# One decoder-block kernel, seven edits joined: input preparation, norm steps, scaled rows, `w_down` rows, strided transposes, and a wait at the seam to the experts

## The chip, the cores and the metric

The kernel runs on one core of a Trainium2 chip. The time is device microseconds (us) of one execution; a measurement is the median of several runs. A profile is one execution of its own, recorded instruction by instruction. Engines: PE is TensorE, DVE is VectorE, ACT is ScalarE, POOL is GpSimd, SP issues most DMAs. ACT and POOL issue some too.

## What is computed

One decoder layer on x of 1024 tokens by 1024 channels, all in float32:

```python
h = rms_norm(x, attn_norm_g)
proj = h @ w_in                                   # 1024 x 4608: conv, q, k, v, two gates
conv_out = silu(layer_norm(conv31(a * sigmoid(gate))))       # 512 channels, 31 taps
attn_out = rms_norm((softmax(q1 k1) - lam * softmax(q2 k2)) @ v)   # 4 heads, causal
merged = gates[0] * (conv_out @ w_conv_out) + gates[1] * (attn_out @ w_attn_out)
x = x + merged @ w_out
h2 = rms_norm(x, ffn_norm_g)
# router: best of 4 groups, best 2 of its 8 experts; so 2048 rows spread over 32 experts
for e in range(32):
    y[rows_e] += w_e * ((silu(h2[rows_e] @ w_gate[e]) * (h2[rows_e] @ w_up[e])) @ w_down[e])
return x + y
```

Each expert has 6 MB of weights (`w_gate`, `w_up`, `w_down`, 2 MB each), 201 MB in all.

## The kernel before

Every large matmul is done on operands cut in two: `split` (L92) writes a high part on ACT (L93) and the rest on DVE (L94), and `mm3` multiplies three times (L98 to L100). So PE runs three matmuls for each product, and every operand costs an ACT and a DVE instruction.

**Input preparation and attention.** x comes in eight tiles of 128 tokens. For each tile, ACT squares it (`prep_a`, L194), DVE takes the inverse root in a chain of small instructions (`rsqrt`, L65 to L75), POOL multiplies the tile by the gain (`prep_g`, L202), DVE scales an identity by the inverse root (`prep_s`, L207), and PE multiplies the tile by that diagonal, which transposes and scales it at once (`prep_b`, L218, two groups of four blocks). A loop over units U (4 heads x 8 tiles and seven more) then projects one tile (24 matmuls into `pq`) and interleaves scores and values of earlier units. The order on PE and ACT is the order of the code in this part; a string `plan` says where the transposes of the next tile (`p`, `P`) stand among the eight projection steps (digits). In the first unit, POOL also makes the low parts of two of the four weight chunks. ACT evacuates the end of a projected tile into `rq` (L269).

**Convolution and gates.** The 31 taps run on DVE while PE does the gates. Between the gates stand the steps of the layer norm: `norm_stats` (four groups of transposes, L615) and `norm_silu` (four groups, L632), for each half of the tokens, through a ring of two PSUM tiles that ACT empties.

**Output projection and routing.** For two halves of 512 columns and eight token tiles, PE projects into `px`, DVE adds the residual (L801), POOL multiplies by the gain (`scaled`, L815, into `uu`), and an ACT DMA writes `uu` to DRAM as `h2d`. `scaled` also permutes the columns (it reads every fourth one), so that the gathered rows later match the weights' layout. In the second half the router runs in groups of tiles: a chain of some 35 DVE instructions whose `oh`, `ohb` (L956, L957) PE needs (L961). DVE also makes the low part `ml` of the next tile.

**Seam and experts.** The last group gives `idx` (L999). Then POOL gathers each expert's rows (L1002, an indirect DMA whose descriptors POOL writes), PE transposes them (`x_front`, L1013), and for each expert: gate and up projections, `hidden`, a transpose of the result (`hid_t`, L1041), the down projection and a scatter-add (L1055). Weights come by 1 MB DMAs on SP's queue (`chunk_dma`, L1066) into a ring of 12 buffers, with at most five loads in flight once the ring has been filled; ACT and DVE split each buffer (`ch` 1.92 us, `cl` 2.29 us), which frees it. A chunk of `w_gate` or `w_up` is one piece of 8 KB for each partition, a chunk of `w_down` two pieces of 4 KB.

Of the kernel before, what the change touches and what calls it, by code (L numbers as in the profile page):

```python
# [49 lines left out]
class Block:  # L50
# [132 lines left out]

    def xload(self, tb):
        xf = self.i["x"].rearrange("o t d -> (o t) d")
        self.nc.sync.dma_start(self.xts[:, tb % 4], xf[tb * P:(tb + 1) * P])

    def prep_a(self, *tbs):
        nc, xp = self.nc, self.xp
        n = len(tbs)  # L190
        ss = xp.tile([P, 2], F32, name="ss", bufs=3)[:, :n]
        rr = xp.tile([P, 2], F32, name="rr", bufs=3)[:, :n]
        for u, tb in enumerate(tbs):
            nc.scalar.activation(self.xmisc[:, 1], self.xts[:, tb % 4], AF.Square, accum_out=ss[:, u:u + 1])  # L194
        self.rsqrt(xp, rr, ss, n, 1.0 / D, f"xn{n}")
        for u, tb in enumerate(tbs):
            self.xr[tb] = rr[:, u:u + 1]

    def prep_g(self, tb):
        xt = self.xts[:, tb % 4]  # L200
        self.xg[tb] = xg = xt if tb else self.xmisc[:, 3]
        self.nc.gpsimd.tensor_tensor(xg, xt, self.gb, op=ALU.mult)  # L202

    def prep_s(self, tb):
        c = (tb % 2) * P
        self.dg[tb] = dg = self.xmisc[:, 3, c:c + P] if tb else self.xmisc[:, 2, 7 * P:]
        self.nc.vector.tensor_scalar(dg, self.ident, self.xr[tb], None, op0=ALU.mult)  # L207
# [5 lines left out]
    def prep_b_(self, tb, kk):  # L213
# [19 lines left out]
    def attention(self):  # L233
# [169 lines left out]
        with tc.manual_schedule(engines={E_.PE, E_.Activation}):  # L403
            self.xload(0)
            nc.sync.dma_start(self.gb, row_bcast(i["attn_norm_g"], D))
            wload(0, 0)
            self.xload(1)
            wload(0, 1)
            wload(0, 2)
            self.xload(2)  # L410
            wload(0, 3)
            self.xload(3)
            self.consts_load()
            self.xr, self.xg, self.dg = {}, {}, {}
            self.prep_g(0)
            self.prep_a(0)
            self.prep_s(0)
            self.prep_a(1)
            self.prep_g(1)
            wsplit(0, 0)  # L420
            self.prep_b(0, 0)
            self.prep_b(0, 4)
            self.prep_s(1)
            wsplit(0, 1, nc.gpsimd)
            wsplit(0, 2)
            self.prep_a(2)
            self.prep_g(2)
            wsplit(0, 3, nc.gpsimd)
            for U in range(NU + 7):
# [16 lines left out]
                if pj:  # L446
# [3 lines left out]
                    if h == 0 and tb + 4 < NT:  # L450
                        self.xload(tb + 4)
                    if h == 0 and 0 < tb < NT - 1:
                        self.prep_s(tb + 1)
# [38 lines left out]
                plan = "0p12cP3a4qk56Q7" if nxt else "012c3a4qk5Q67"  # L492
                for c in plan:
                    if c.isdigit():
                        step(int(c))
                    elif c == "p" and nxt:
                        self.prep_b(nxt, 0)
                        if U == 0:
                            self.prep_a(3)
# [22 lines left out]
                    elif c == "k" and U == 1:  # L522
# [83 lines left out]
    def norm_stats(self, th):  # L606
        nc, cv = self.nc, self.cv
        mv = cv.tile([P, 4, 2], F32, name="mv", bufs=2)
        z = [self.yp.tile([P, KW - 1 + T], F32, name="yy", bufs=2) for _ in range(2)]
        self.zs = zs = [z[t // 2][:, t % 2 * 512:(t % 2 + 1) * 512] for t in range(4)]  # L610
        for t, zt in enumerate(zs):
# [4 lines left out]
            nc.scalar.activation(zt, pt.rearrange("p a b -> p (a b)"), AF.Copy)  # L616
            st = cv.tile([P, 6], F32, name="st", bufs=2)
            nc.vector.bn_stats(st, zt)
            nc.vector.bn_aggr(mv[:, t], st)
        rr = cv.tile([P, 4], F32, name="crr", bufs=2)  # L620
        self.rsqrt(cv, rr, mv[:, :, 1], 4, 1.0, "cn")
        for t in range(4):
            nc.vector.tensor_scalar(zs[t], zs[t], mv[:, t, 0:1], rr[:, t:t + 1], op0=ALU.subtract, op1=ALU.mult)

    def norm_silu(self, th):
        nc = self.nc
        sl = slice(th * 512, (th + 1) * 512)
        for cb in range(NCB):
# [66 lines left out]

    def merge_conv(self, fills, stop, steps):
# [4 lines left out]
        for j in range(ND - 2):  # L701
            Wg = self.gate_load(CG0 + j * P)
            for th in range(2):
                self.gate(Wg, th, s2[th][:, j])
            self.pin = self.last_split
            self.fill(fills if j + 1 < stop else 99)
            for f, th in steps.get(j, ()):
                f(th)
        Wg = [self.gate_load(CG0 + j * P) for j in (ND - 2, ND - 1)]
        for th in range(2):  # L710
            for q in range(2):
                self.gate(Wg[q], th, s2[th][:, ND - 2 + q])
            if th == 0:
                for f, t in steps.get(ND - 1, ()):
                    f(t)
# [14 lines left out]
        for th in range(2):  # L730
            for j in range(ND):
                if th == 0 and j + 2 < ND:
                    Wo.append(wload(j + 2))
                if (th, j) == (0, 2):
                    self.norm_split(1)
# [3 lines left out]
                nc.vector.tensor_tensor(mg, mg, sg, op=ALU.add)  # L739

# [27 lines left out]
    def out_proj(self):  # L768
# [5 lines left out]
        for n in range(2):  # L774
# [6 lines left out]
            for tb in range(NT):  # L781
# [24 lines left out]
                self.scaled(uu, xt, gb2)  # L806
# [5 lines left out]

    def scaled(self, uu, xt, gb2):
        by = lambda a: a.rearrange("t (p k) -> t k p", k=4)
        self.nc.gpsimd.tensor_tensor(uu.rearrange("t (k p) -> t k p", k=4), by(xt), by(gb2), op=ALU.mult)  # L815

    def out_last(self, px, mh, ml, W, xt, prev, gb2):
# [30 lines left out]
        self.scaled(uu, xt, gb2)  # L848
# [473 lines left out]
```

## Time and profile before

| what | value |
|---|---|
| median of three runs | 1435.72 us (1428.46 to 1436.32) |
| the profiled execution | 1441.21 us |
| its span, first to last instruction | 1439.5 us |
| PE, DVE, ACT, POOL busy | 94%, 76%, 55%, 17% of the span |
| mean granted TensorE clock | 0.975 of full |

The shares are averages over stages with different limits. The stages, in us from the start: preparation and attention to about 330, convolution and gates to about 670, output projection and routing to 822, the seam to 850, the experts to 1401, and a tail. DMA is hardly used in the first half and 96% busy in the experts.

### The profile page before, as it was taken

Reading aid. Unit: us, or ns where it says so; the run is one execution under the profiler, and the core shown is the slowest. Engines: PE = TensorE matmul, PEld = TensorE weight load, DVE = VectorE, ACT = ScalarE, POOL = GpSimd, SP = SyncE. Lnnn points to the kernel's source line nnn. Section 1 sums busy time; section 2 is a strip of 40 time slices with the busy share of each in tenths; the row PEclk is TensorE's granted clock in tenths of the full one; section 3 lists DMA queues with packets and bytes.
Section 4 is the critical chain, followed back from the end, with each engine's and each line's share of the span. In section 5 each row is a group of like instructions: output and inputs, shape, how many; then the busy total and the mean of one; then the engine's idle time right before and its main releaser. Section 6 shows DMA issues by size and latency. Waiting matters only on the chain.

```text
span 1439.5 us, 18415 instructions
## 1 busy us (share of the span) xinstructions
PE 1349.0 (94%) x6854; PEld 1136.7 (79%) x6854; DVE 1087.7 (76%) x1402; ACT 788.2 (55%) x1109; POOL 240.6 (17%) x349
## 2 busy tenths in 40 slices
PE   5899999999999999899988589999999999999995
PEld 5899999888888888778767468888888887777774
DVE  7776776645789895565575869999998888888893
ACT  4466675653111112531342258888888777777782
POOL 4322121200000000000232211111111212222211
PEclk9999999999999999999997889999999999999997
DMA  5110100102111121043942189999999999999981
GB/s 180 35 45 12 34 18 18 30 27 77 51 44 40 49 59 44 1 130 117 325 158 96 48 297 352 358 371 377 363 370 368 366 368 360 359 361 362 349 326 17
DMA packets 105789, 264.81 MB, mean 184 GB/s; under 512 B 14033, under 2 KB 59234, under 8 KB 89314
## 3 DMA queue, kind: packets, MB, share of 16 engines
q1 hardware_dynamic: 89218, 237.73, 44.8%
q0 software_dynamic: 9216, 16.81, 4.8%
q10 hardware_dynamic: 7264, 9.08, 1.8%
q8 instruction: 55, 0.90, 0.2%
q14 instruction: 36, 0.29, 0.1%
HBM read 255.18 MB, written 25.17 MB: 195 GB/s over the span
## 4 chain that ended last, share of the span: by engine, by line
PE 39%; issue 31%; DMA 11%; DVE 7%; POOL 7%; ACT 3%; POOLq 0%; SPq 0%; ACTq 0%; DVEq 0%
DMA out_dram<-y,idx 8%; PE pg L99 4%; PE pg L98 4%; PE pg L100 4%; POOL out_dram L1055 3%; POOL gx L1002 2%; PE pq L98 2%; PE pq L100 2%; PE pq L99 2%; PE po L363 2%; PE pc L98 2%; PE pc L100 2%; PE pc L99 2%; PE pb L98 2%; PE pb L99 2%
## 5 line engine op out<-in xcount | busy, mean ns | idle before, releaser
L94 DVE TENSOR_TENSOR cl<-ra,ch 128x2048 fp32r<-128x2048 f32 x192 | 436.1, 2289 | 69.6 <-ACT ch L93 69.0
L93 ACT ACTIVATE ch<-ra 128x2048 fp32r<-128x2048 f32 x192 | 365.2, 1920 | 94.7 <-DMA ra<-in_w_gate_e_dram 39.1
L99 PE MATMUL pg<-cl,xh 128*128 128x512 f32 x512 | 203.8, 398 | 4.8 <-DVE cl L94 4.8
L98 PE MATMUL pg<-ch,xh 128*128 128x512 f32 x512 | 203.8, 398 | 3.7 <-ACT ch L93 2.1
L100 PE MATMUL pg<-ch,xl 128*128 128x512 f32 x512 | 201.8, 394 | 0.1
L597 DVE SCALAR_TENSOR_TENSOR ac<-yy,dw,ac 128x1024 f32<-128x1024 f32 x120 | 153.1, 1283 | 2.3
L99 PEld LDWEIGHTS pg<-cl,xh 128*128 128x128 f32 x512 | 96.9, 189 | 27.1 <-DVE cl L94 7.5
L98 PEld LDWEIGHTS pg<-ch,xh 128*128 128x128 f32 x512 | 97.2, 190 | 26.1 <-ACT ch L93 4.1
L100 PEld LDWEIGHTS pg<-ch,xl 128*128 128x128 f32 x512 | 96.9, 189 | 20.5 <-DVE xl L94 0.9
L98 PE MATMUL py<-ch,dh 128*128 128x512 f32 x256 | 103.0, 402 | 1.9 <-ACT dh L93 1.9
L1055 POOL DMA_INDIRECT out_dram<-y,idx x32 | 66.0, 2063 | 226.1 <-ACT y L1054 202.8
L99 PE MATMUL py<-cl,dh 128*128 128x512 f32 x256 | 101.5, 397 | 0.0
L100 PE MATMUL py<-ch,dl 128*128 128x512 f32 x256 | 101.3, 396 | 0.0
L98 PE MATMUL pg<-hTh,whb 128*128 128x512 f32 x256 | 100.1, 391 | 0.0
L100 PE MATMUL pg<-hTh,wlb 128*128 128x512 f32 x256 | 99.8, 390 | 0.0
L99 PE MATMUL pg<-hTl,whb 128*128 128x512 f32 x256 | 99.8, 390 | 0.0
L1002 POOL DMA_INDIRECT gx<-h2d,idx x32 | 53.9, 1685 | 265.5 <-PE pt L1013 226.1
L98 PE MATMUL pq<-wha,hTh 128*128 128x384 f32 x256 | 95.7, 374 | 0.0
L100 PE MATMUL pq<-wha,hTl 128*128 128x384 f32 x256 | 86.8, 339 | 0.8 <-DVE hTl L94 0.8
L93 ACT ACTIVATE whb<-wrb 128x512 fp32r<-128x512 f32 x48 | 30.0, 631 | 104.3 <-PE pg L99 86.1
L99 PE MATMUL pq<-wla,hTh 128*128 128x384 f32 x256 | 86.9, 339 | 0.0
L332 ACT ACTIVATE ee<-sc,mx 128x128 f32<-128x128 f32 (+7 forms) x64 | 47.1, 745 | 22.5 <-DVE mx L330 22.5
(308 smaller groups left out, 2766.3 us busy)
## 6 DMA issues: line engine op xcount, KB each, us to landing
ra<-in_w_gate_e_dram SPq DMA_DIRECT2D x64, 1024.0 KB
ra<-in_w_up_e_dram SPq DMA_DIRECT2D x64, 1024.0 KB
ra<-in_w_down_e_dram SPq DMA_DIRECT2D x64, 1024.0 KB
wrb<-in_w_in_dram SPq DMA_DIRECT2D x32, 256.0 KB
wra<-in_w_in_dram SPq DMA_DIRECT2D x32, 192.0 KB
xts<-in_x_dram SPq DMA_DIRECT2D x8, 512.0 KB
wrb<-in_w_in_dram SPq DMA_DIRECT2D x32, 128.0 KB
wor<-in_w_out_dram SPq DMA_DIRECT2D x8, 512.0 KB
```

Of the source, the lines that this page charges most:

```text
L93: self.nc.scalar.activation(hi, src, AF.Copy)
L94: self.last_split = (eng or self.nc.vector).tensor_tensor(lo, src, hi.bitcast(F32), op=ALU.subtract).ins
L98: mm(ps, lhsT=lh, rhs=rh, start=first, stop=False)
L99: mm(ps, lhsT=lh, rhs=rl, start=False, stop=False)
L100: mm(ps, lhsT=ll, rhs=rh, start=False, stop=last)
L332: nc.scalar.activation(ee[:, :n], sc[:, :n], AF.Exp, bias=mx, accum_out=s["sm"][qb][:, c:c + 1])
L363: nc.tensor.matmul(po, lhsT=s["at"][j // 4][:, j % 4], rhs=s["V"][j], start=j == 0, stop=j == qb)
L597: nc.vector.scalar_tensor_tensor(ac, yy[:, j:j + T], w(j), ac, op0=ALU.mult, op1=ALU.add)
L1002: self.nc.gpsimd.indirect_dma_start(out=gx, out_offset=None, in_=self.h2d, in_offset=bass.IndirectOffsetOnAxis(ap=idx, axis=0), bounds_che ...
L1055: nc.gpsimd.indirect_dma_start(out=self.out, out_offset=bass.IndirectOffsetOnAxis(ap=idx, axis=0), in_=y, in_offset=None, bounds_check=T - ...
```

## The change

Seven edits:

1. **Preparation.** The gain and the inverse root are applied to the x tile by one DVE instruction, in two halves for the first two tiles; `prep_s` is gone, and PE transposes the tile with a plain identity. POOL has no work here any more; the two weight splits that it did go to DVE. A fifth slot for x tiles is used, the loads are reordered, and the plans of the first two units put the next tile's transposes later.
2. **Constants.** `consts_late` runs one unit later.
3. **Norm steps.** `norm_stats` and `norm_silu` are cut in halves of two PSUM tiles, and each half stands behind another gate (or, for the last two, behind a product of the output weights).
4. **Scaled rows.** `uu` is a plain DVE multiplication, so `h2d` is stored in column order.
5. **Strided transposes.** `x_front` therefore reads every fourth column of the gathered rows.
6. **`w_down`.** Its chunks are loaded as one piece of 8 KB for each partition, and `hid_t` reads every second column to match.
7. **Seam.** POOL writes a small tile right behind the first gather, DVE copies it, and DVE's first weight splits stand behind that copy.

```diff
     def prep_g(self, tb):
-        xt = self.xts[:, tb % 4]
-        self.xg[tb] = xg = xt if tb else self.xmisc[:, 3]
-        self.nc.gpsimd.tensor_tensor(xg, xt, self.gb, op=ALU.mult)
-    def prep_s(self, tb):
-        self.dg[tb] = dg = self.xmisc[:, 3, c:c + P] if tb else self.xmisc[:, 2, 7 * P:]
-        self.nc.vector.tensor_scalar(dg, self.ident, self.xr[tb], None, op0=ALU.mult)
+        w = D // 2 if tb < 2 else D
+        for c in range(0, D, w):
+            x = self.xslot(tb)[:, c:c + w]
+            g = self.nc.vector.scalar_tensor_tensor(x, x, self.xr[tb], self.gb[:, c:c + w], op0=ALU.mult, op1=ALU.mult)
+        return g.ins
...
-            nc.tensor.matmul(pt[:, k], lhsT=self.xg[tb][:, (kk + k) * P:(kk + k + 1) * P], rhs=self.dg[tb],
-                             start=True, stop=True)
+            nc.tensor.transpose(pt[:, k], self.xslot(tb)[:, (kk + k) * P:(kk + k + 1) * P], self.ident)
...
             self.xload(0)
+            wload(0, 0)
             nc.sync.dma_start(self.gb, row_bcast(i["attn_norm_g"], D))
-            wload(0, 0)
+            wload(0, 1)
             self.xload(1)
-            wload(0, 1)
             wload(0, 2)
             self.xload(2)
+            self.xload(3)
             wload(0, 3)
-            self.xload(3)
+            self.xload(4)
...
+                if U < 2:
+                    plan = ("012345p67P", "0123p45P67")[U]
...
-        b.merge_conv(6, 4, {4: [(b.norm_stats, 0)], 5: [(b.norm_silu, 0), (b.norm_stats, 1)],
-                            ND - 1: [(b.norm_silu, 1)]})
+        b.merge_conv(6, 4, {8: (b.norm_stats, 0, 0), 9: (b.norm_stats, 0, 1), 11: (b.norm_silu, 0, 0), 12: (b.norm_silu, 0, 1),
+                            13: (b.norm_stats, 1, 0), 14: (b.norm_stats, 1, 1), 17: (b.norm_silu, 1, 0),
+                            19: (b.norm_silu, 1, 1)})
...
-                self.scaled(uu, xt, gb2)
+                nc.vector.tensor_tensor(uu, xt, gb2, op=ALU.mult)
...
+            g = gx[:, k0 * P:(k0 + 4) * P].rearrange("t (p k) -> t k p", k=4)
             for k in range(4):
-                nc.tensor.transpose(pt[:, k], gx[:, (k0 + k) * P:(k0 + k + 1) * P], self.ident)
+                nc.tensor.transpose(pt[:, k], g[:, k], self.ident)
...
-                nc.tensor.transpose(pt[:, k], sg[:, c * P:(c + 1) * P], self.ident)
+                g = sg[:, c // 2 * 2 * P:(c // 2 + 1) * 2 * P].rearrange("t (p k) -> t k p", k=2)
+                nc.tensor.transpose(pt[:, k], g[:, c % 2], self.ident)
...
-        wd = i["w_down_e"][0, e].rearrange("(k p) f -> p k f", p=P)
+        wd = i["w_down_e"][0, e].rearrange("(c p k) f -> c p (k f)", p=P, k=2)
...
-            self.gather(col(k), gx[k])
+            first = self.gather(col(k), gx[k])
+        tok = [mp.tile([P, 1], F32, name=f"tok{k}") for k in range(2)]
+        with tc.issue_after(first.ins):
+            nc.gpsimd.memset(tok[0], 0.0)
+        seen = nc.vector.tensor_copy(tok[1], tok[0])
         S[0]["raw"] = raw0
-        S[0]["wg"] = sum([self.chunk_split(r) for r in raw0[0]], [])
+        with tc.issue_after(seen.ins):
+            S[0]["wg"] = sum([self.chunk_split(r) for r in raw0[0]], [])
```

PE at the very start, before and then after (`pt` is the transposed tile, `wha` and `wla` the weight parts, `hTh` and `hTl` the input's):

```order
L218 MATMUL pt<-xmisc 128x128 x8
L98 MATMUL pq<-wha,hTh 128x384
L99 MATMUL pq<-wla,hTh 128x384
L100 MATMUL pq<-wha,hTl 128x384
L218 MATMUL pt<-xmisc,xts 128x128 x4
```

```order
L98 MATMUL pq<-wha,hTh 128x384
L99 MATMUL pq<-wla,hTh 128x384
L100 MATMUL pq<-wha,hTl 128x384
L218 MATMUL pt<-ident,xts 128x128 x4
L98 MATMUL pq<-wha,hTh 128x384
```

Before, the second tile's first transposes stand behind one projection step; now six steps stand ahead of them (the rows of the after kernel are the last of those six).

DVE in the output projection, at the router's second group, before and then after (`wro` is the x tile after the residual, `ei` and `ef` the chosen experts, `ml` the low part of the next tile):

```order
L953 MAX_INDEX ei<-e_7145,off 128x8 x2
L801 TENSOR_TENSOR wro<-wro,px 128x512
L954 CAST ef<-ei 128x4
L966 TENSOR_TENSOR dl<-e_7145 128x2
L94 TENSOR_TENSOR ml<-mg_4025,mh 128x1024
L956 TENSOR_TENSOR oh<-io_6342,ef 128x128
L957 TENSOR_TENSOR ohb<-oh 128x64
```

```order
L806 TENSOR_TENSOR wro<-wro,px 128x512
L954 MAX_INDEX ei<-e_7139,off 128x8 x2
L811 TENSOR_TENSOR uu<-wro,gb_6784 128x512
L955 CAST ef<-ei 128x4
L967 TENSOR_TENSOR dl<-e_7139 128x2
L94 TENSOR_TENSOR ml<-mg_4019,mh 128x1024
L957 TENSOR_TENSOR oh<-io_6336,ef 128x128
L958 TENSOR_TENSOR ohb<-oh 128x64
```

The multiplication into `uu` now stands on DVE between the residual and the one-hot rows.

DVE at the seam, before and then after:

```order
L999 TENSOR_SCALAR idx<-ptb 128x32
L992 COPY tbl<-ptb 128x96
L94 TENSOR_TENSOR cl<-ra,ch 128x2048 x2
L94 TENSOR_TENSOR xl<-pt,xh 128x512 x2
L94 TENSOR_TENSOR cl<-ra,ch 128x2048 x4
```

```order
L1000 TENSOR_SCALAR idx<-ptb 128x32
L993 COPY tbl<-ptb 128x96
L1105 COPY tok_7627<-tok_7626 128x1
L94 TENSOR_TENSOR cl<-ra,ch 128x2048 x2
L94 TENSOR_TENSOR xl<-pt,xh 128x512 x2
```

The copy of `tok` stands ahead of the first two splits; on POOL the write of `tok` stands between the first and the second gather.

## Rows read from the trace of the kernel before

**Rows 1.** Busy time of each engine in stretches of the run (us, then the busy us and the number of instructions of PE, PEld, DVE, ACT and POOL), the granted TensorE clock as a share of full, the busy share of the DMA engines and their GB/s: second half of the output projection, then the experts in two parts.

```profile
735.00:822.00 87.00, 69.28 (x386) 57.33 (x384) 60.24 (x231) 19.73 (x42) 21.73 (x10) 0.85 0.25 84
...
850.00:1110.00 260.00, 260.00 (x1223) 215.51 (x1222) 233.78 (x165) 208.59 (x159) 42.63 (x29) 0.99 0.96 361
1110.00:1401.00 291.00, 282.71 (x1314) 228.23 (x1313) 249.67 (x158) 224.22 (x173) 65.12 (x30) 1.00 0.98 359
```

**Rows 2.** The first 30 us in order of time: start, duration, engine, line, operation; in brackets how long the engine had been idle and what ended that.

```profile
6.85 2.34 POOL L202 TENSOR_TENSOR xmisc<-xts,xmisc 128x1024 f32<-128x1024 f32 x1 [5.00 <-DMA xmisc<-in_attn_norm_g_dram]
...
7.10 2.10 DVE L75 SCALAR_TENSOR_TENSOR xn1y<-xn1t,xn1y 128x1 f32<-128x1 f32 x1
...
10.25 3.75 PE L218 MATMUL pt<-xmisc 128*128 128x128 f32 x16 [10.25 <-DVE xmisc L207]
...
17.39 2.26 DVE L207 TENSOR_SCALAR xmisc<-ident,rr 128x128 f32<-128x128 f32 x1
...
17.55 0.84 ACT L93 ACTIVATE wha<-wra 128x768 fp32r<-128x768 f32 x1 [0.41 <-DMA wra<-in_w_in_dram]
...
19.79 2.05 PE L218 MATMUL pt<-xmisc,xts 128*128 128x128 f32 x8 [3.58 <-DVE xmisc L207]
...
28.07 0.38 ACT L269 ACTIVATE rq<-pq 128x256 f32<-128x256 f32 x1 [2.04 <-PE pq L100]
...
28.39 1.05 PE L218 MATMUL pt<-xmisc,xts 128*128 128x128 f32 x8
```

**Rows 3.** The same view in the experts: one expert's `x_front`.

```profile
846.82 1.03 PE L1013 MATMUL pt<-ident,gx 128*128 128x128 f32 x8
```

**Rows 4.** The page's groups of instructions: DVE's three-operand instruction on 1024 columns (number, then busy us and mean ns of one).

```profile
L597 DVE SCALAR_TENSOR_TENSOR ac<-yy,dw,ac 128x1024 f32<-128x1024 f32 x120 | 153.1, 1283 | 2.3
```

**Rows 5.** POOL's multiplications by line (shortest, median and longest ns of one): L202 reads 1024 neighbouring columns, L815 512 columns in steps of four.

```profile
L202 POOL TENSOR_TENSOR xts<-xts,xmisc x7: 2344/2376/2392, 11.1 to 52.3; 128x1024 f32<-128x1024 f32 x7
```

**Rows 6.** The same view, L815.

```profile
L815 POOL TENSOR_TENSOR uu<-wro,gb x16: 2102/2112/3362, 677.0 to 813.9; 128x512 f32<-128x512 f32 x16
```

**Rows 7.** PE's transposes into `pt` from 570 to 625 us: what they waited for (us in total, times).

```profile
  ACT ac L637: 4.7, 6
  ACT yy L616: 0.6, 1
```

**Rows 8.** Waits from 735 to 822 us: who waited for whom, us in total, times, longest.

```profile
PE pr L961 <- DVE ohb L957: 11.5, 4, 5.6
...
PE pt L863 <- DVE wro L801: 3.1, 3, 1.6
```

**Rows 9.** Two stretches behind such waits, columns as in the first group.

```profile
757.00:763.00 6.00, 6.00 (x21) 4.84 (x19) 2.82 (x8) 0.60 (x1) 0.00 (x0) 0.54 0.26 88
...
779.00:790.00 11.00, 10.79 (x40) 9.29 (x40) 2.81 (x11) 1.75 (x3) 0.07 (x1) 0.53 0.40 144
```

**Rows 10.** DVE and then POOL in order of time, 741 to 757 us.

```profile
745.08 3.15 DVE L94 TENSOR_TENSOR ml<-mg,mh 128x1024 fp32r<-128x1024 f32 x1
...
754.03 2.20 DVE L956 TENSOR_TENSOR oh<-io,ef 128x128 f32<-128x128 f32 x1
...
753.98 2.10 POOL L815 TENSOR_TENSOR uu<-wro,gb 128x512 f32<-128x512 f32 x1 [6.83 <-DVE ef L954]
```

**Rows 11.** The end of the routing and the seam in order of time.

```profile
813.86 2.29 POOL L815 TENSOR_TENSOR uu<-wro,gb 128x512 f32<-128x512 f32 x1 [11.26 <-DVE wro L832]
...
814.23 1.93 DVE L932 TENSOR_TENSOR st<-fss 128x1 f32<-128x1 f32 x1
...
823.49 0.19 DVE L999 TENSOR_SCALAR idx<-ptb 128x32 int32<-128x32 f32 x1 [1.26 <-PE ptb L987]
...
824.00 4.49 DVE L94 TENSOR_TENSOR cl<-ra,ch 128x2048 fp32r<-128x2048 f32 x2 [0.16 <-ACT ch L93]
824.58 2.81 POOL L1002 DMA_INDIRECT gx<-h2d,idx  x1 [8.44 <-DVE tbl L992]
826.32 2.53 SPq L1066 DMA_DIRECT2D ra<-in_w_gate_e_dram  x2
...
832.49 1.94 PE L1013 MATMUL pt<-ident,gx 128*128 128x128 f32 x8 [9.03 <-DMA gx<-h2d,idx]
...
834.70 0.99 POOL L1002 DMA_INDIRECT gx<-h2d,idx  x1 [5.32 <-PE pt L1013]
...
838.05 2.49 SPq L1066 DMA_DIRECT2D ra<-in_w_up_e_dram  x2
```

**Rows 12.** The weights' DMA queue in four short stretches (packets, MB, time of the packets as a share of 16 engines' time): 712 to 716 and 840 to 844 us, in which nearly all data packets have 8 KB, then 782 to 784 and 846 to 850 us, in which they have 4 KB.

```profile
q1 hardware_dynamic: 219, 1.66, 103.1%
...
q1 hardware_dynamic: 192, 1.44, 94.9%
...
q1 hardware_dynamic: 204, 0.83, 101.8%
...
q1 hardware_dynamic: 323, 1.25, 82.8%
```

**Rows 13.** Waits in the second part of the experts, 1110 to 1430 us.

```profile
ACT ch L93 <- DMA ra<-in_w_gate_e_dram: 39.1, 22, 5.4
```

**Rows 14.** All transposes of gathered rows: ns of one, first and last start.

```profile
L1013 PE MATMUL pt<-ident,gx x256: 269/273/445, 832.5 to 1385.2; 128*128 128x128 f32 x128
```

More of the change, by code (lines that the diff above doesn't have):

```diff
@@ L521, in attention @@
                             qkt_b(*qk, 1)
[L522 removed]
+                    elif c == "k" and U == 2:
                         self.consts_late(self.ps)
@@ L604, in fill, with norm_stats @@
         del self.taps[:n]
-    def norm_stats(self, th):
+    def norm_stats(self, th, u):
         nc, cv = self.nc, self.cv
[L608 to L611, printed above, removed]
+        if u == 0:
+            self.mv = cv.tile([P, 4, 2], F32, name="mv", bufs=2)
+            z = [self.yp.tile([P, KW - 1 + T], F32, name="yy", bufs=2) for _ in range(2)]
+            self.zs = [z[t // 2][:, t % 2 * 512:(t % 2 + 1) * 512] for t in range(4)]
+        mv, zs = self.mv, self.zs
+        for t in (2 * u, 2 * u + 1):
             pt = self.psT.tile([P, 4, P], F32, name="pt", tag="T", bufs=2)
@@ L694, in merge_attn, with norm_step @@
             pass
+    def norm_step(self, n, steps):
+        if n in steps:
+            f, th, u = steps[n]
+            f(th, u)
+            if (f, th, u) == (self.norm_silu, 1, 1):
+                self.norm_split(1)
     def merge_conv(self, fills, stop, steps):
@@ L700, in merge_conv @@
         Wg = {}
[L701 to L715, printed above, removed]
+        order = [(j, th) for j in range(ND - 2) for th in range(2)]
+        order += [(j, th) for th in range(2) for j in (ND - 2, ND - 1)]
+        for n, (j, th) in enumerate(order):
+            if j < ND - 2 and th == 0 or (j, th) == (ND - 2, 0):
+                for q in ((j,) if j < ND - 2 else (j, j + 1)):
+                    Wg[q] = self.gate_load(CG0 + q * P)
+            self.gate(Wg[j], th, s2[th][:, j])
+            if th == 1 and j < ND - 2:
+                self.pin = self.last_split
+                self.fill(fills if j + 1 < stop else 99)
+            self.norm_step(n, steps)
+            if (j, th) == (ND - 1, 0):
                 self.norm_split(0)
@@ L739, in merge_conv @@
                 nc.vector.tensor_tensor(mg, mg, sg, op=ALU.add)
+                if th == 0:
+                    self.norm_step(16 + j, steps)
     def out_load(self, n):
@@ L1001, in gather @@
     def gather(self, idx, gx):
-        self.nc.gpsimd.indirect_dma_start(out=gx, out_offset=None, in_=self.h2d,
-                                          in_offset=bass.IndirectOffsetOnAxis(ap=idx, axis=0),
-                                          bounds_check=T - 1, oob_is_err=False)
+        return self.nc.gpsimd.indirect_dma_start(out=gx, out_offset=None, in_=self.h2d,
+                                                 in_offset=bass.IndirectOffsetOnAxis(ap=idx, axis=0),
+                                                 bounds_check=T - 1, oob_is_err=False)
     def x_front(self, gx):
@@ L1084, in load_raw @@
         wu = i["w_up_e"][0, e].rearrange("(c p k) f -> c p (k f)", p=P, k=4)
[L1085 to L1088 removed]
+        wd = i["w_down_e"][0, e].rearrange("(c p k) f -> c p (k f)", p=P, k=2)
+        return ([self.chunk_dma(wg[c], F) for c in range(2)], [self.chunk_dma(wu[c], F) for c in range(2)],
+                [self.chunk_dma(wd[c], D) for c in range(2)])
     def experts(self):
@@ L1187, in overflow @@
             for src, st in ((wg, 4), (wu, 4), (wd, 2)):
-                for k in range(0, 2 * st, st):
+                for c in range(2):
                     raw = mp.tile([P, 2048], F32, name="oraw", bufs=6)
                     raw = raw.rearrange("p (a b) -> p a b", b=2048 // st)
-                    part = src[k // st][:, bass.ds(er, 1)][:, 0] if st == 4 else src[:, bass.ds(er, 1)][:, 0, k:k + st]
-                    nc.sync.dma_start(raw, part)
+                    nc.sync.dma_start(raw, src[c][:, bass.ds(er, 1)][:, 0])
                     raws.append(raw)
```

70 lines of the change are left out of this document (29 added, 41 removed).

## The prediction

> **What bounds the kernel now.** I read the busy table by stretches first, then the idle time of PE by what ended it, then the order of instructions around each idle stretch. PE is busy for 94% of the span, so a gain can come from four places only: the rest of PE's idle time, PE's own work, stretches at a low granted clock, and the ends. The first 10.25 us pass before PE has anything to do; it then waits 3.58 us for the second tile's diagonal, and the first projected tile is evacuated at 28.07 [rows 2]. In the norm steps PE waits 5.3 us for ACT to empty the two PSUM tiles [rows 7]. In the second half of the output projection it waits 11.5 us for one-hot rows, 5.6 of them in the last route, and 3.1 us for the residual [rows 8]; the clock of that stretch is 0.85 in the mean [rows 1] and 0.54 and 0.53 in two pieces of 6 and 11 us behind such waits [rows 9], that is, the 1.2 GHz level for nearly all of them. At the seam PE stands for 9.03 us [rows 11]. In the first part of the experts it is busy for 260.0 of 260.0 us, although DMA is 0.96 busy; in the second part it loses 291 − 282.7 = 8.3 us [rows 1], where ACT waits for loads 22 times [rows 13]. So the weights limit only the later experts.
>
> A second thing is to be seen in the order of instructions: small DVE instructions that lie beside a POOL multiplication last about as long as that. The last step of the inverse root takes 2.10 us beside a POOL instruction of 2.34 [rows 2], `oh` 2.20 beside one of 2.10, `ml` 3.15 [rows 10], `st` 1.93 beside one of 2.29; `idx`, with POOL idle, takes 0.19. The other way round, the first gather's descriptors take POOL 2.81 us beside two DVE splits and 0.99 for a later gather [rows 11]. Four of the seven edits take POOL and DVE apart.
>
> **The change part by part**, against the profiled execution of 1441.2 us. It lies 5.5 us above the median of 1435.72; I take the differences over unchanged.
>
> **Start.** POOL's multiplication and its cover of 2.1 us over the inverse root go, and so does the diagonal (2.26 us for the second, which ended PE's wait of 3.58) [rows 2]. DVE gets a three-operand instruction per tile: 1.28 us for 1024 columns [rows 4], 0.64 for a half. It also gets two low weight parts; two of 2048 columns take 4.49 [rows 11], so one of 768 takes 0.84. SP's order puts a weight chunk ahead of the gain, which can hold the first multiplication back by that transfer, about a microsecond; the inverse root is 2 us earlier, so tile 0's transposes start near the old time. What is new is that nothing of tile 1 stands between the eight projection steps. The tile can end when the fourth chunk is split: its load ended ACT's wait at 17.55, the split takes 0.84 [rows 2] and the low part another 0.84, which makes 19.2, and two steps of three short matmuls after that make 20.5 to 21.5, against 28.07: −7. Of this a part is only moved: tile 1's transposes come later, at 1 to 2 us for a group, and tile 2's DVE multiplication now lies behind splits, so I keep 3. To this comes PE's own work: a group of four blocks with the diagonal takes 1.05 us when warm [rows 2], eight plain transposes 1.03 [rows 3], 0.53 less for each group, so 12 groups of tiles 2 to 7 give −6.3. Together −9; if the moved part comes back whole, −4, and if all 7 are kept, −13. The later constants have no user nearby and cost nothing; if one waited, PE would stand for that load once.
>
> **Norm steps.** The cut steps do the same instructions; behind each half a gate's matmuls run on PE while ACT empties two tiles. The wait of 5.3 us in sum [rows 7] goes but for the first tile of a half: −4.5. Bounds: −5.3, and 0 if each half meets ACT with older work in its queue.
>
> **Scaled rows.** POOL loses 2.1 us for each tile and half [rows 6]; DVE gets a multiplication of 512 columns, for which I take half of 1283 ns [rows 4], rounded up to 0.7 for a tile just written. That is 16 × 0.7 = 11 us more on an engine that was busy for 60 of the 87 us of this stretch [rows 1]; in return the stretched pieces shrink: `oh` by about 2, `ml` by at least 1 [rows 10]. In each of the three inner router groups the chain shortens by 2 and grows by at most 0.7 where the new instruction stands ahead of `oh`. The waits outside the last route are 3.1 + (11.5 − 5.6) = 9.0 us [rows 8]; I take 5 of them. The 17 us at about half clock [rows 9] hold some 9 us of work at full clock, so 8 us are to be had if PE no longer stands before them; I take 2. Together −7. Bounds: −15 (nearly all of 17), and +2, the 11 us of new work less 9 of waits. In the last route `st` falls from 1.93 towards 0.2 and the new multiplication of 0.7 stands ahead: −1.1 (−0.5 to −1.5).
>
> **Strided transposes.** PE's count is unchanged; what a stride of four, or of two in `hid_t`, does to PE's reading no row of before shows. POOL shows it for itself: 2376 ns for 1024 neighbouring columns [rows 5], 2112 for 512 in steps of four [rows 6], so 1.78 times as long per element. A PE transpose takes 1.03/8 = 0.129 us [rows 3]. Bounds: 0, if PE takes one column in its time wherever it lies (a gain has no source), and 0.10 us for each by POOL's ratio. I take 0: the read belongs to the loading of an operand, a row of its own on PE that runs beside the matmul, and POOL is another engine; the price stays as a rival. The Trainium skill (SBUF — State Buffer, section "Door 1: The DMA port swizzle") speaks against this edit: memory lines have 16 bytes, and an access needs at least two hits in a line for full bandwidth, so four-byte elements in steps of four get one hit, in steps of two just two. By it the gathered rows' eight transposes would pay and `hid_t`'s four would not; by my reading neither does.
>
> **`w_down`.** A third of the weights comes in pieces of 8 KB instead of 4. The rows disagree on what that gives: 8 KB stretches take 1.031 × 64 / 1.66 = 39.7 and 42.2 us of packet time for each MB, 4 KB ones 39.2 and 42.4 [rows 12], so from 7% quicker to 7% slower. On a third of 291 us, 7% is 6.8 us, and PE's idle time of 8.3 caps a gain; the whole run of 31 periods takes 552.7 us [rows 14]. I take −4, half of the cap, since half as many packets can hardly cost more for a byte; bounds 0 and −8. The Trainium skill (the same page, section "A bandwidth-pool intuition that's wrong") gives about 358 GB/s between the memory and a core, which the experts' 359 and 361 [rows 1] already reach; by that the term would be 0 and the sum 4 us poorer. Against it, 1.66 MB pass in 4 us in one stretch [rows 12], which is 415 GB/s.
>
> **Seam.** The first gather's descriptors shrink from 2.81 towards 0.99 [rows 11], so `x_front`, for which PE waits, starts up to 1.8 us earlier. The wait put on DVE is priced so: behind the copy stand the first splits, the low part of `x_front` and four more splits, and for these wait PE's first gate matmuls and SP's next loads, whose buffers they free. Two splits of 4.49 us that began at 824.00 now begin near 826, so the first two loads (826.32) go out some 2 us later; the third, at 838.05, lies behind `x_front` [rows 11] and comes no later. Bounds −1.8 and +2 (if the delayed loads are what the later experts lack); I take −1.
>
> **Sum:** −9 − 4.5 − 7 − 1.1 − 4 − 1 = −26.6, so 1414.6 against the profiled 1441.2, and 1409 against the median.
>
> **Rivals.** *Weak form.* The clock pieces and half of the projection's waits stay (−2 instead of −7) and `w_down` gives nothing: 1435.7 − 9 − 4.5 − 2 − 1.1 − 1 = 1418, with a start at its lower bound 1423; 1415 to 1428. For it: DMA at 0.98 and 359 GB/s. Against it: the stretched rows are plain.
>
> *DVE becomes the bound.* DVE takes what POOL did: 8 × 1.28 at the start and 11 us in the projection. If the start gives 4, the norm steps 1, the projection costs 2, the seam and the route nothing, and `w_down` its 4, the time is 1429 (1425 to 1433). Against it: DVE was busy for only 69% of the projection.
>
> *Strided reading, slower than before.* One mechanism, at every operand load of gathered rows and of `hid_t`: 12 × 32 = 384 transposes. Without `w_down`'s gain, which a slower PE hides, I start from 1413. PE's idle time of 8.3 us in the later experts takes up that much. At POOL's ratio 384 × 0.10 = 38.4, less 8.3, gives 1443; at doubled transposes 384 × 0.129 = 49.5, less 8.3, 1454. So it decides from about 0.10 us for each. With only the eight of `x_front` paying POOL's ratio it is 1430. For it: POOL's rows. Against it: POOL's ratio is another engine's. The Trainium skill's rule on 16-byte lines (the page and section above) would make it likelier for `x_front` alone.
>
> *The seam's wait does nothing:* gather unchanged, loads later; 1409 + 3 = 1412, inside the forecast.
>
> **How the numbers follow.** What a measurement of this kernel can tell from no change is about 0.5%, or 7 us: faster is below 1428.5, slower above 1443. Forecast 1409 (1396 to 1422, from the terms' bounds taken together, not all at one end): 0.66, all faster. Weak form: 0.17, all faster but for a hundredth. DVE bound: 0.08, a quarter of it faster, the rest the same. Strided reading: 0.09, 0.06 slower and 0.03 the same or just faster. That makes faster 0.84, same 0.10, slower 0.06. The range 1394 to 1432 takes in the forecast, the weak form and most of the DVE case; the sum of all best bounds is further down, but they will not meet.
>
> **What would show it.** Right: the first `rq` near 21 us; PE's groups of L218 at half their time; no POOL multiplication before the seam; waits for ACT in the norm steps under 1 us; `oh` near 0.2 us and the two clock pieces gone; the first gather's descriptors near 1 us and `x_front` 1 to 2 us nearer behind `idx`; `x_front`'s eight transposes still at 1.03 us; PE idle in the later experts about 4 us. Wrong: tile 2's transposes waiting for DVE, PE waiting for `wro` longer than before, or transposes at 0.2 us. What would make the prediction wrong as a whole is a slower read of strided rows, or a clock that falls in other places because PE's first steps now wait for weight chunks one at a time.

## The result and the profile after

The changed kernel takes 1391.51 us (median of four runs, 1390.40 to 1395.52), the kernel before 1433.07 (four runs, 1428.46 to 1436.32): a ratio of 0.9717, 95% interval 0.9680 to 0.9755. The direction was forecast; the gain of 41.6 us was forecast as 26.6, and the time lies 2.5 us below the range. The profiled execution after has a span of 1388.7 us, 50.8 less than that of before. That one, at 1441.21 us, lay 8 us above the median of its kind, so the differences of the two traces are some 9 us larger in all than those of the medians.

Where the work stands in the two traces (us; start of the instruction named):

| place | before | after | moved by | forecast for the step to it |
|---|---|---|---|---|
| first `rq` | 28.07 | 21.10 | −7.0 | |
| last `rq` | 283.50 | 275.12 | −8.4 | −9 |
| first gate | 346.53 | 336.41 | −10.1 | 0 |
| first `px` | 670.46 | 651.67 | −18.8 | −4.5 |
| first residual of the second half | 736.26 | 712.67 | −23.6 | −7 with the next row |
| last residual | 813.31 | 769.86 | −43.5 | |
| `idx` | 823.49 | 779.21 | −44.3 | −1.1 |
| first `x_front` | 832.49 | 784.74 | −47.8 | −1 |
| end of the span | 1439.5 | 1388.7 | −50.8 | −4 |

The busy table by stretches (columns as in [rows 1]): of before the second half of the output projection alone; of after the norm steps and that half.

```profile
736.30:812.90 76.60, 65.72 (x360) 54.63 (x359) 51.54 (x190) 18.58 (x38) 19.45 (x9) 0.87 0.26 85
```

```profile
566.00:605.00 39.00, 39.00 (x193) 32.68 (x192) 18.91 (x57) 16.12 (x28) 0.80 (x4) 1.00 0.04 12
...
712.70:769.80 57.10, 55.28 (x353) 47.54 (x353) 43.49 (x195) 18.75 (x38) 1.84 (x2) 1.00 0.32 113
```

PE is never idle in the norm steps. In the second half of the projection the clock is 1.00 instead of 0.87; PE is busy for 10.4 us less with the same matmuls and idle for 1.8 us instead of 10.9. Of the two kinds of wait in [rows 8] PE has, up to the end of the routing, only this left, 4.4 us of it in the last route:

```profile
PE pr L962 <- DVE ohb L958: 4.7, 2, 4.4
PE pt L864 <- DVE wro L806: 1.4, 1, 1.4
```

The start and the seam in order of time (as in [rows 2, 11]):

```profile
16.64 0.84 ACT L93 ACTIVATE wha<-wra 128x768 fp32r<-128x768 f32 x1 [2.19 <-DMA wra<-in_w_in_dram]
...
21.10 0.38 ACT L268 ACTIVATE rq<-pq 128x256 f32<-128x256 f32 x1
...
24.09 0.63 PE L218 MATMUL pt<-ident,xts 128*128 128x128 f32 x4 [1.41 <-DVE rr L75]
...
36.88 0.45 PE L218 MATMUL pt<-ident,xmisc 128*128 128x128 f32 x1 [3.03 <-DVE nlam L165]
...
779.21 0.19 DVE L1000 TENSOR_SCALAR idx<-ptb 128x32 int32<-128x32 f32 x1 [1.26 <-PE ptb L988]
...
780.30 1.24 POOL L1003 DMA_INDIRECT gx<-h2d,idx  x1 [24.66 <-DVE tbl L993]
...
781.77 4.48 DVE L94 TENSOR_TENSOR cl<-ra,ch 128x2048 fp32r<-128x2048 f32 x2
...
784.08 2.53 SPq L1067 DMA_DIRECT2D ra<-in_w_gate_e_dram  x2
784.74 1.95 PE L1015 MATMUL pt<-ident,gx 128*128 128x128 f32 x8 [5.56 <-DMA gx<-h2d,idx]
```

The fourth weight chunk again sets the first tile, as forecast. At the seam the gather's descriptors take 1.24 us instead of 2.81, and its rows land 3.2 us behind them instead of 5.1: the second part was not in the sum.

### The profile page after: what moved, and what is told of

It reads as the page before. It is cut to its first block, busy times and chain, and to the rows that moved or that the text cites. A ratio compares the mean times of both kernels' runs of the same rounds, so it can differ in the third digit from the quotient of the medians.

```text
span 1388.7 us, 18243 instructions
## 1 busy us (share of the span) xinstructions
PE 1322.6 (95%) x6790; PEld 1126.3 (81%) x6790; DVE 1059.4 (76%) x1423; ACT 787.1 (57%) x1109; POOL 169.2 (12%) x324
## 4 chain that ended last, share of the span: by engine, by line
PE 45%; issue 31%; DMA 9%; DVE 7%; POOL 6%; ACT 2%; POOLq 0%; SPq 0%; DVEq 0%; ACTq 0%
DMA out_dram<-y,idx 7%; PE pg L98 5%; PE pg L99 5%; PE pg L100 5%; POOL out_dram L1058 3%; POOL gx L1003 2%; PE pq L98 2%; PE pq L99 2%; PE pq L100 2%; PE po L362 2%; PE pb L98 2%; PE pb L99 2%; PE pb L100 2%; PE pc L98 2%; PE pc L100 2%
## 5 line engine op out<-in xcount | busy, mean ns | idle before, releaser
L99 PEld LDWEIGHTS pg<-cl,xh 128*128 128x128 f32 x512 | 96.8, 189 | 22.3 <-DVE cl L94 3.1
L1003 POOL DMA_INDIRECT gx<-h2d,idx x32 | 49.3, 1539 | 289.0 <-PE pt L1015 224.4
L1058 POOL DMA_INDIRECT out_dram<-y,idx x32 | 56.4, 1764 | 226.4 <-ACT y L1057 202.8
```

Source lines behind the costliest of these rows:

```text
L99: mm(ps, lhsT=lh, rhs=rl, start=False, stop=False)
L1003: return self.nc.gpsimd.indirect_dma_start(out=gx, out_offset=None, in_=self.h2d, in_offset=bass.IndirectOffsetOnAxis(ap=idx, axis=0), bou ...
L1058: nc.gpsimd.indirect_dma_start(out=self.out, out_offset=bass.IndirectOffsetOnAxis(ap=idx, axis=0), in_=y, in_offset=None, bounds_check=T - ...
```

## The experiments

Times are medians; differences are against the changed kernel's 1391.51 us. The kernel before gave medians of 1432.0 to 1437.1 us beside these kernels, so one or two microseconds say nothing; and the runs of kernels 3 to 4.4 us above the changed one still overlap with those of that one (1390.40 to 1395.52), so that there the traces carry the reading. Stage lengths are from the traces.

**Scaled rows: contention or order.** Edits 4 and 5 undone:

```diff
-nc.vector.tensor_tensor(uu, xt, gb2, op=ALU.mult)
+self.scaled(uu, xt, gb2)        # GpSimd, permuted
...
-    nc.tensor.transpose(pt[:, k], g[:, k], self.ident)
+    nc.tensor.transpose(pt[:, k], gx[:, (k0 + k) * P:(k0 + k + 1) * P], self.ident)
```

> Edits 4 and 5 undone together: GpSimd makes the scaled rows and permutes them, x_front reads neighbouring columns. From the two traces the output projection (first px to last px) fell from 142.4 to 118.2 us, of which 19.4 in its second half. If these rows are the cause, the projection takes 138 to 143 us here, the experts' period falls from 17.84 to 17.73 us, and the time is 1391.5 + 20 to 25 - 2 to 3.5 = 1408 to 1415. Rival: the projection's gain comes from the other edits (norm steps that no longer leave work behind); then it stays near 120 us and the time is 1388 to 1392.

1412.57 us, +21.1. The projection takes 134.9 us, between the two: its second half (first to last residual) 70.9 us, against 57.6 in the changed kernel and 77.5 in the kernel before; its first (first residual to the first of the second half) 59.1, against 55.3 and 60.1. But with the edit PE's order changed too, the ranking matmuls `pr` standing later. So GpSimd's work alone was put back beside an unchanged order:

```diff
+if n == 1:   # a tile that nobody reads
+    dd = ep.tile([P, 512], BF, name="dd", bufs=1)
+    nc.gpsimd.tensor_tensor(dd.rearrange("t (k p) -> t k p", k=4), by(xt), by(gb2), op=ALU.mult)
```

> The changed kernel, and in the second half of the projection GpSimd also makes its old multiplication (512 columns in steps of four) into a tile that nobody reads. PE, DVE and ACT run in exactly the order of the changed kernel. Theory A (contention): VectorE's small instructions stretch to 2 us again, PE waits 2 us for the one-hot rows, the clock falls, and most of the 19.4 us come back: 1402 to 1411, with stretches at 0.5 to 0.6 of the clock. Theory B (order): the waits went because the scheduler put PE's ranking matmuls later behind the one-hot rows; then DVE's pieces stretch but PE waits little: 1391 to 1396, clock 1.00.

1409.97 us, +18.5, and 17.7 of it in this half (57.6 to 75.3 us). One group in order of time:

```profile
750.15 2.11 POOL L817 TENSOR_TENSOR dd<-wro,gb 128x512 bf16<-128x512 f32 x1 [6.53 <-DVE wro L806]
750.26 2.55 DVE L811 TENSOR_TENSOR uu<-wro,gb 128x512 f32<-128x512 f32 x1
752.74 0.16 DVE L959 CAST ef<-ei 128x4 f32<-128x4 uint32 x1
...
754.33 0.23 DVE L962 TENSOR_TENSOR ohb<-oh 128x64 bf16<-128x64 f32 x1
...
754.60 0.19 PE L966 MATMUL pr<-ohb,ltri 128*128 128x32 bf16 x1 [2.25 <-DVE ohb L962]
```

`uu` takes 2.55 us beside GpSimd instead of 0.69, the chain to `ohb` comes 2 us late, and PE waits 2.25. The waits of this half are back, and the clock of the 6 us behind that one is 0.50, the 1.2 GHz level:

```profile
PE pr L966 <- DVE ohb L962: 10.6, 4, 4.4
PE pt L868 <- DVE wro L806: 5.9, 3, 3.2
```

```profile
754.60:760.60 6.00, 6.00 (x27) 5.42 (x26) 1.87 (x9) 0.00 (x0) 0.00 (x0) 0.50 0.63 221
```

Theory A stands; the order of PE was not the cause. The same with a third of GpSimd's time (256 neighbouring columns):

> The same with a quarter to a third of the GpSimd time (256 neighbouring columns, some 0.6 us) in each tile of the second half. Theory A: VectorE's pieces beside it stretch to 0.6 us instead of 2; PE's waits stay under a microsecond and the clock stays up: 1391 to 1396. If any collision is enough to pull the clock down: 1400 or more. Theory B: 1391 to 1393.

1395.94 us, +4.4; in the trace this half is 3.0 us longer. The GpSimd pieces took 0.74 us, PE's one wait for `wro` was 1.96 us, and the clock stayed at 1.00. So in these two runs the cost grows faster than GpSimd's time: at 0.74 us a piece the chain mostly hides it, at 2.1 it does not, and the clock comes on top. The edit alone, on the kernel before:

> The kernel before with edits 4 and 5 alone (scaled rows on VectorE, strided transposes of the gathered rows). If the projection's contention is a cost by itself, the projection falls by 20 to 24 us and the experts' period rises by 0.09 us, 1433 - 24 + 3 = 1411 to 1415. If the gain needs the norm steps' edit as well (less left over for VectorE when the projection begins), 1418 or more.

1418.77 us, a ratio of 0.9871 (0.9816 to 0.9927). That is 18.3 us below the kernel before beside it (1437.11), at the lower end of the 18 to 22 expected; the time itself is above 1415, since the kernel before was 4 us slower here than the 1433 reckoned with. In the traces the projection falls from 142.4 to 122.0 us and the span by 22.3. The first half does not get shorter (59.4 us for 60.1). It did not stay short without these two edits either (59.1 in the first run above), so its 4.8 us take these edits and another one together.

**Strided transposes.** DVE makes the permuted rows, so that `x_front` reads neighbouring columns:

```diff
-nc.vector.tensor_tensor(uu, xt, gb2, op=ALU.mult)
+self.scaled(uu, xt, gb2, nc.vector)
...
```

> VectorE makes the scaled rows, but reads them in steps of four, so that x_front reads neighbouring columns as before. PE, DVE and ACT keep the order of the changed kernel. If strided reading is what lengthened the experts' period by 0.11 us, x_front's eight transposes go back to 1.03 us and the period to 17.76 (hid_t keeps its stride), 1389 to 1391 in all; if VectorE's strided read costs it as much as it cost GpSimd (1.78 times, 16 x 0.5 us), the projection is 1 to 5 us longer: 1391 to 1396. Rival: the period stays at 17.84 because something else (the 8 KB rows of w_down) sets it.

1394.70 us, +3.2. `uu` takes 1.12 us instead of 0.69, and the projection is 3.4 us longer; the early period (from one expert's `x_front` to the next) falls from 17.84 to 17.77 us. Loads and matmuls of `x_front`, after and then here (ns, shortest, median, longest):

```profile
L1015 PEld LDWEIGHTS pt<-ident,gx x256: 196/211/226, 784.7 to 1335.7; 128*128 128x128 f32 x128
L1015 PE MATMUL pt<-ident,gx x256: 270/283/457, 784.7 to 1335.8; 128*128 128x128 f32 x128
```

```profile
L1018 PEld LDWEIGHTS pt<-ident,gx x256: 137/140/231, 789.5 to 1340.4; 128*128 128x128 f32 x128
L1018 PE MATMUL pt<-ident,gx x256: 270/272/447, 789.6 to 1340.6; 128*128 128x128 f32 x128
```

Strided reading does cost the load half as much again (211 for 140 ns), but PE overlaps it: 11 ns are left for each transpose, a tenth of the rival's price.

**`w_down`.** Edit 6 undone:

```diff
-wd = i["w_down_e"][0, e].rearrange("(c p k) f -> c p (k f)", p=P, k=2)
+wd = i["w_down_e"][0, e].rearrange("(k p) f -> p k f", p=P)
...
```

> The changed kernel with edit 6 undone: w_down in two pieces of 4 KB for each partition, hid_t reads neighbouring columns. PE, DVE and ACT keep their order. Theory A (longer pieces shorten the loads): the stretch from the twentieth x_front to the last scatter, 253.7 us after and 257.0 before, is 2 to 4 us longer again, 1391.5 + 1 to 3 = 1392.5 to 1394.5. Theory B (the bytes bound it): it stays at 253 to 254, and the early periods fall by 4 x 11 ns = 0.04 us from 17.84 to 17.80: 1390 to 1391.5.

1392.47 us (1392.06 to 1398.96), +1.0, not to be told from nothing. From the first `x_front` to the end it takes 603.5 us, after 604.0; the period is 17.80. Theory B: the longer pieces gave nothing, and `hid_t`'s stride took 0.04 us an expert:

```profile
L1043 PEld LDWEIGHTS pt<-ident,sg x128: 138/139/143, 810.1 to 1368.8; 128*128 128x128 f32 x128
L1043 PE MATMUL pt<-ident,sg x128: 270/272/328, 810.3 to 1368.9; 128*128 128x128 f32 x128
```

```profile
L1044 PEld LDWEIGHTS pt<-ident,sg x128: 195/196/219, 808.2 to 1366.8; 128*128 128x128 f32 x128
L1044 PE MATMUL pt<-ident,sg x128: 270/282/388, 808.4 to 1366.9; 128*128 128x128 f32 x128
```

**The seam's wait.** Edit 7 removed:

```diff
...
-with tc.issue_after(seen.ins):
-    S[0]["wg"] = ...
+S[0]["wg"] = ...
```

> The changed kernel without edit 7: VectorE's first weight splits do not wait. Theory A (the wait is worth what the seam showed): the first gather's descriptors take 2.8 us again instead of 1.24, x_front starts 9.0 us behind idx instead of 5.6, the time is 1391.5 + 3.5 = 1395. Rival: the later experts are limited by their loads, which leave 2 us earlier without the wait, and give most of it back: 1390 to 1392.5.

1395.41 us (1392.77 to 1402.65), +3.9; in the trace `x_front` comes 9.2 us behind `idx` instead of 5.5, and the span is 2.4 longer. And the loads held back instead of the splits (SP's first load into a freed buffer waits for GpSimd's small write behind the gather):

> The splits go at once, but SP's first load into a freed buffer waits until GpSimd has written the first gather's descriptors. It tells the two parts of the seam's gain apart: before, the gather's descriptors took 2.81 us and its rows landed 5.1 us after them; after, 1.24 and 3.2. If the landing is slowed by the two loads that leave at the same time, the descriptors take 2.8 us here and the landing 3.2, x_front 7.2 to 7.5 us behind idx. If the landing does not depend on the loads, it takes 5 us and x_front comes 9 us behind idx, as without any wait.

```profile
781.41 0.19 DVE L1000 TENSOR_SCALAR idx<-ptb 128x32 int32<-128x32 f32 x1 [1.26 <-PE ptb L988]
782.50 2.82 POOL L1003 DMA_INDIRECT gx<-h2d,idx  x1 [24.47 <-DVE tbl L993]
785.47 1.30 SPq L1067 DMA_DIRECT2D ra<-in_w_gate_e_dram  x2
...
788.54 1.74 PE L1015 MATMUL pt<-ident,gx 128*128 128x128 f32 x7 [7.17 <-DMA gx<-h2d,idx]
```

The descriptors take 2.82 us again, yet the rows land 3.2 us behind them. So the 3.7 us at the seam have two parts: 1.6 from descriptors written without DVE beside them, 2.1 from weight loads that no longer leave ahead of the gather: here SP sends the first of them 0.15 us behind the end of the descriptors (785.32), in the run without any wait it does so 1.1 us before (781.47, the descriptors end at 782.56). The time, 1393.19 us (1390.37 to 1394.95), is too near to tell.

**Norm steps whole, at their old places** (the same steps in one piece each, at gates 9, 11 and 13):

> The changed kernel with the layer norm's steps whole and at their old places. The stretch from the first gate to the first px fell from 323.9 to 315.3 us. Theory A: the waits for ACT (5.3 us) and a clock below full behind them (0.97 over 49 us, with cold transposes) both come back, 7 to 9 us: 1398 to 1401. Theory B: only the waits themselves were worth something, 4 to 5.5 us: 1395.5 to 1397.

1401.47 us, +10.0. PE's waits there:

```profile
PE pt L633 <- ACT ac L638: 3.7, 4, 1.2
...
PE pt L615 <- ACT ac L638: 1.4, 2, 0.7
PE pt L615 <- ACT yy L616: 0.6, 1, 0.6
```

Gates and products are 9.8 us longer, 5.7 of them these waits; the clock from 552 to 663 us is 0.98. The first half of the projection is 4.2 us longer too: PE waits 2.3 us for the split of the second half's first weights, at 0.72 of the clock behind it. That wait is in the kernel before (2.0 us at 732) and not in the changed one. Theory A, and more: the edit also gives the 4 us of the projection's first half. How, was not tried; the first run of the scaled rows, with the norm steps as changed, loses 3.8 of them too.

**Old start** (all edits but 1 and 2):

> All edits but 1 and 2: the input preparation of before (GpSimd's multiplication, the scaled identity, the old loads and plans). The last rq fell by 8.4 us and the first gate by 10.1. If the start stands by itself, both come back: 1391.5 + 8 to 10 = 1400 to 1402, and the stages behind it keep their lengths. Rival: what was gained at the start is absorbed later (VectorE's taps, loads): 1392 to 1397.

1401.57 us, +10.1. The last `rq` comes 5.7 us later, not 8.4, mostly since the second tile's first transposes waited 1.48 us here, not 3.58; PE's wait for a product of the branch grows from 1.05 to 2.65 us, with the clock at 0.72 behind it, and the first `px` is 8.9 us late. The start stands by itself; its size varies with what the clock does later.

Undone one at a time, the parts add up to 21.1 + 10.0 + 10.1 + 3.9 + 1.0 = 46.1 us, 4.5 more than the whole gain of 41.6. The 4 us of the projection's first half, which two of these runs bring back, are in that sum twice.

**A faster version, in two steps.** First, tile 4's multiplication ahead of the step that waits for GpSimd (PE's 3.03 us at 36.88):

```diff
-self.prep_g(tb + 2)
+g = self.prep_g(tb + 2)
+if tb == 2:
+    st["pin"] = g        # dd stands behind it
```

> An attempt at a faster version: in the changed kernel PE waits 3.0 us for tile 4's transposes at 36.9 us, since VectorE stands 2 us for GpSimd's part of an inverse root (qrr) with tile 4's multiplication queued behind that step. Here that step (dd) is queued behind tile 4's multiplication; PE and ACT keep their order. If the wait is what holds PE, the fourth and later projected tiles come 2 to 3 us earlier and the time is 1388.5 to 1390. If dd then comes late for the scores, the gain is lost there: 1391 to 1392.5.

1389.36 us (1386.28 to 1392.45), not to be told from the changed kernel. The wait falls to 0.38 us and 2.0 us are gained up to 203 us; at the first gate they are gone. Both kernels have a wait of PE's at 275 us, for ACT, which itself waits some 5 us for a load of convolution weights while `rq` is queued behind it. The 7 us behind that wait, in the changed kernel and here:

```profile
276.00:283.00 7.00, 7.00 (x44) 6.20 (x45) 4.34 (x11) 3.48 (x11) 2.88 (x12) 1.00 0.14 40
```

```profile
274.30:281.30 7.00, 6.93 (x34) 5.89 (x35) 3.50 (x10) 3.49 (x11) 2.85 (x12) 0.76 0.14 40
```

After a wait of 2.08 us the clock stayed up in the one, after 2.51 it fell in the other; in the run with the old `w_down` it was 0.76 after 2.11. So that split was put behind the evacuation:

```diff
-nxt = [part(0, q) for q in range(ND // 2)]
-yield
+nxt = [part(0, q) for q in range(ND // 2 - 1)]
+yield
+nxt.append(part(0, ND // 2 - 1))
```

> A version that should beat both: tile 4's multiplication first, as above, and one split moved. In every run PE waits 2.1 to 2.5 us at about 276 us for ACT's evacuation of the last projected tile, which stands on ACT behind the fourth split of the first convolution weights, and that split waits 5 us for its load. In some runs the clock of the 6 us behind this wait is 0.72, in others 1.00, though the wait is the same; that moved all later stages by 1.7 us or not, and ate the 2.0 us that the version above had gained up to there. Here the split stands behind the evacuation. If ACT's queue is what PE waits for, the wait goes, the clock stays at 1.00 there in every run, and the gate stage begins at 332 to 333 us against 336.3: 1386 to 1388. If PE then waits for the fourth weight chunk itself, 1 us of it stays: 1388 to 1389.5.

1385.21 us (six runs, 1384.30 to 1388.82), a ratio of 0.9671 (0.9641 to 0.9701) to the kernel before, and 6.3 us below the changed one: its slowest run lies below the fastest of that. `rq` no longer waits, PE's wait for ACT is gone (1.1 us for a low weight part, which the changed kernel has too, stays), the clock is 1.00 there, and the gates begin at 332.2:

```profile
267.28 0.39 ACT L268 ACTIVATE rq<-pq 128x256 f32<-128x256 f32 x1
...
272.22 0.63 ACT L93 ACTIVATE whb<-wrb 128x512 fp32r<-128x512 f32 x1 [2.57 <-DMA wrb<-in_w_in_dram]
```

```profile
276.00:283.00 7.00, 7.00 (x47) 6.19 (x46) 4.41 (x7) 3.67 (x11) 0.00 (x0) 1.00 0.01 2
```

## Why the prediction was wrong in size

**Scaled rows: the step that failed.** The sum took 7 us: 5 of 9.0 us of waits and "2" of the 8 us that the low clock held. The second half alone gave 19.9 (23.6 to 43.5 in the table). The mechanism was right, as the dummy multiplication shows: GpSimd's 2.1 us beside an otherwise unchanged kernel bring 18.5 us back. What was mis-sized is what follows from a wait. Nearly all of the waits went (9.0 in [rows 8], 1.7 after, without the last route), and so did both low stretches [rows 9] and what lay between: of the 19.9 us some 9 are idle time (10.9 to 1.8) and some 10 PE's own work at the higher clock. The prediction priced the two parts as separate chances when they are one: with the wait gone, there is nothing left for the clock to fall behind. The bound of −15 was too near as well. DVE's price, 0.7 us a tile, was right (0.69), and nothing of it was seen on PE.

**Norm steps: right mechanism, half the size.** The waits were 5.3 us and went. Not counted were the clock behind them and the 4.8 us in the projection's first half, of which undoing this edit brings 4.2 back and undoing the scaled rows 3.8: they take both.

**Seam: one part missing.** Descriptors gave 1.6 us of the up to 1.8 foreseen; the collision of the gather's rows with weight loads, 2.1 us, was not seen, although [rows 11] show the load leaving at 826.32, before the descriptors end at 827.39, and the rows landing only at 832.49. The delayed loads, priced as a loss of up to 2 us, were the gain.

**`w_down`: nothing.** Half of PE's idle time was a choice without a row behind it. The 415 GB/s set against the lower price came from a short window: it counts packets that run past its end, so that their time is 103.1% of it. The ten us around it have 362 GB/s (kernel before):

```profile
710.00:720.00 10.00, 9.82 (x51) 8.00 (x51) 3.84 (x2) 2.58 (x5) 2.10 (x1) 1.00 1.00 362
```

The Trainium skill (SBUF — State Buffer, section "A bandwidth-pool intuition that's wrong (but worth ruling out)") has about 358 GB/s between the memory and a core, by which this term was 0. The run agrees: the stretch from the first `x_front` to the end takes 603.5 us with the 4 KB pieces and 604.0 with those of 8 KB. That stretch is still 3.0 us shorter than before (607.0), and the traces hold most of it in two places. From the second to the third `x_front` the clock was 0.89 in the kernel before and 1.00 in the changed one, behind nearly the same wait of PE (1.61 and 1.53 us); from the last `x_front` to the end, 60.5 and 59.2 us, the kernel before has 8 us at 0.79 that the changed one lacks:

```profile
846.82:862.87 16.05, 14.44 (x62) 11.31 (x61) 12.18 (x10) 9.59 (x8) 2.73 (x1) 0.89 0.81 293
...
1417.00:1425.00 8.00, 7.57 (x24) 5.51 (x24) 1.65 (x4) 0.34 (x2) 0.00 (x0) 0.79 0.00 0
```

```profile
799.43:813.90 14.47, 12.94 (x62) 10.46 (x61) 12.22 (x10) 9.60 (x8) 2.65 (x1) 1.00 0.90 330
```

Whether an edit does this stays open: the first of the two is 0.89 both with edits 4 and 5 undone and with these two alone on the kernel before.

**Strided reading: the rival fell.** It needed 0.10 us for each transpose; 0.011 was measured, 0.11 us for an expert or at most 3.5 us in all. The reason given, that the load runs beside the matmul, is what the rows show.

**Start: right in kind.** −8.4 in the traces for −9; the first tile at 21.10 for 20.5 to 21.5. PE's groups of tiles 2 to 7 fell from 1.05 to about 0.60 us, some 5 us for the 6.3 forecast. Of these and the 7.0 at the first tile, waits took back 3 to 4, as reckoned, but not where it was reckoned: 1.41 us ahead of tile 2, which the prediction named as a sign of being wrong, and 3.03 ahead of tile 4, which it did not see. That the sum came out is in part luck. Undoing it costs 10.1 us in the medians. The further 1.7 us between the last `rq` and the first gate are the clock behind the wait at 275 us, which stayed up in this execution and fell to 0.76 over 7 us in that of before.

**Weak form and a bounded DVE** did not occur. The range failed because the rows, the norm steps and the seam were all off on the same side, the first two for one reason: a removed wait was priced by its own length alone.

## What to carry to other kernels

Where PE waits 2 us and its clock is low behind that, price the wait and the slow stretch as one item, and look for every such wait. A GpSimd tensor instruction beside a chain of small DVE ones costs its length on that chain (2 us late beside 2.1 us here); ask who waits at the end of it before calling GpSimd's work hidden. When a gain disappears further on, compare the granted clock behind the next wait before looking for another cause, and take that wait away.

## What the runs showed of the hardware

- The same wait at 274 to 284 us, 2.1 to 2.5 us long, was followed by a clock of 1.00 in seven kernels' traces and of 0.76 over 7 us in six others, though the instructions there are the same. From the last `rq` to the first gate the seven take 61.3 to 61.5 us and the six 62.8 to 63.2. What decides it no run here shows.
- A DVE instruction of 0.69 us took 2.55 beside a GpSimd instruction of 2.11 and ended 0.55 us behind it. The Trainium skill (SBUF — State Buffer, section "Who interferes with whom") has a DVE instruction with two inputs in SBUF contend with a GpSimd instruction that reads SBUF, through a port that is locked and not shared. This row agrees: the GpSimd instruction began first, and most of DVE's own 0.69 us lies behind its end.
- A strided load of an operand costs PE 211 ns at a step of four and 196 at a step of two, against 140; of that 10 to 11 ns reach the matmuls. The Trainium skill (SBUF — State Buffer, section "Door 1: The DMA port swizzle") has two hits in a 16-byte line as enough for full bandwidth. The step of two should then be free; the load's row says it is not.
- Two 1 MB loads, the first of them issued 1.1 us before the end of a gather's descriptors, put off the landing of its 128 rows by 2 us (5.1 to 5.3 us behind the descriptors). With the first issued 0.15 us behind that end, it took 3.2 us, as long as with no load issued until 0.7 us before the landing.
